# The low halves of eight split weight matrices: subtraction on the engines, or an accumulating DMA

## The chip, the cores and the metric

The kernel runs on one core of a Trainium2 chip. The metric is the time of one execution on the device in microseconds, as the median of several runs. A core has five instruction queues that run side by side and meet only through semaphores: PE (TensorE, matmuls), DVE (VectorE), ACT (ScalarE), POOL (GpSimd) and SP (SyncE, which here only issues DMAs). Each queue is worked off in order, so an instruction that waits holds up everything behind it on its engine. POOL and ACT can issue DMAs too. Sixteen DMA engines carry all transfers.

## The reference

One transformer block on 256 tokens of width 1024, all in float32:

```
h    = rms_norm(x, ln1_g)
proj = h @ w_in                          # 1024 x 4096: u, q, k, v (512 each) and two gates (1024 each)
gate_ssm, gate_attn = split(proj[..., 2048:] + b_gate)
y_ssm  = s5_mixer(u, ...);  g = gelu(y_ssm);  y_ssm = g * sigmoid(g @ w_glu + b_glu)
y_attn = moba_attention(q, k, v, rel_bias)
merged = sigmoid(gate_ssm) * (y_ssm @ w_up_ssm) + sigmoid(gate_attn) * (y_attn @ w_up_attn)
x = x + merged @ w_out
x = x + hier_moe(rms_norm(x, ln2_g), ...)   # 32 experts of 1024 x 512 x 1024, top 2
out = rms_norm(x, ln_f_g)
```

The change touches the product that makes the two gates: the last 2048 columns of `w_in`.

## The kernel before

The 4096 columns of `w_in` are cut into 16 units of 256 columns. A unit's raw weights lie in memory as 128 partitions x 8 x 256 (partition, k, column), 1 MB, and come by one DMA on SP's queue into one of two buffers (`raw`). Units 0 to 7 (u, q, k, v) are multiplied as plain float32 (`nat`). Units 8 to 15, the gates, are split: `wh` is the weights rounded to the short float32r format, `wl` is the rest, raw minus `wh`. The activations are split in the same way (`hH`, `hL`). PE then adds three products for each of the 8 k, `wh*hH`, `wh*hL` and `wl*hH`, which together are nearly as exact as float32. For a half unit (128 columns, part b) that is 24 matmuls: first 16 with `wh`, alternating, then 8 with `wl`. So `wl` is wanted last in every half.

`wh` and `wl` have two buffers each (`wtiles`), so unit u+1 is split while unit u is multiplied. In `half_split`, called for part 0 and part 1 of the unit before, one part is one cast and one subtraction of [128, 8, 128], 1024 elements in each partition. A table (`KN["e"]`) says which engine does which: the casts (`w8.0h` and so on) lie on ACT and DVE, the subtractions (`w8.0l`) on POOL nine times and on DVE seven times. Another table (`KN["sp"]`) says before which quarter of the unit's matmuls the split is written down. The program writes every instruction by hand in one order; an engine's queue is that order with the other engines' instructions left out.

Between the quarters three background threads are advanced (`bg()`): the state-space layer (S5, names `scan`, `W1e`, `M1s`, `Thp`, `yp`, `stp`), its preparation on POOL (`E`, `pprep`, `Pe`) and attention (`attA`, `attB`, `sc`, `ptp`, `pv`), and behind these the gelu. All are finished before the GLU product, which stands between unit 14 and unit 15. After unit 15 come the up projections, the output projection, the routing, and then the experts: 192 pieces of 1 MB of expert weights (`wslot`) run through 21 buffers, and 32 tokens' places of four experts are multiplied at a time. SP issues the pieces in order, each as soon as its buffer is free; the first ones already while the gate units run (`pump`).

Line 691 is the cast in the helper `copy`, line 694 the subtraction in the helper `tt`, line 1269 the matmuls of the gate units, 1108 and 1110 the state-space output, 1070 the state matmuls, 1361 the attention transposes, 1425 the GLU, 1395 to 1405 the gelu.

Of the kernel before, what the change touches and what calls it, by code (L numbers as in the profile page):

```python
# [11 lines left out]
F32R = mybir.dt.float32r  # L12
# [3 lines left out]
AF = mybir.ActivationFunctionType  # L16
OP = mybir.AluOpType
# [5 lines left out]
KD = 8  # L23
# [622 lines left out]
def hybrid_block(ctx, tc, x_ch, x_tok, small, consts, bc, w_in, w_glu, w_up, w_out, rel, onehot, w_rt, w13, w2,  # L646
                 ln_f, out, dbg=None):
    nc = tc.nc
    V, A, G, T, DS = nc.vector, nc.scalar, nc.gpsimd, nc.tensor, nc.sync
# [9 lines left out]
    def blk(i, name, dt=F32):  # L659
        return blocks.tile([128, 2048], dt, tag=f"r{i}", name=name)  # L660

    def carve(t, *shapes):
        res, o = [], 0
        for sh in shapes:
            n = int(np.prod(sh))
            v = t[:, o:o + n]
            names = "abcdef"[:len(sh)]
            if len(sh) > 1:
                v = v.rearrange("p (%s) -> p %s" % (" ".join(names), " ".join(names)), **dict(zip(names, sh)))
            res.append(v)  # L670
            o += n
        assert o <= t.shape[1]
        return res
# [11 lines left out]
    def pick_engine(name, default, opts):  # L685
        OPTS[name] = (default, opts)
        return engines[KN["e"].get(name, default)]

    def copy(name, out_, in_, default="A", opts="AV"):
        e = pick_engine(name, default, opts)  # L690
        (A.copy if e is A else e.tensor_copy)(out_, in_)  # L691

    def tt(name, out, in0, in1, op, default="V", opts="VG"):
        pick_engine(name, default, opts).tensor_tensor(out=out, in0=in0, in1=in1, op=op)  # L694
# [13 lines left out]
    def split(name, raw, wh, wl, scale=None, psum=False):  # L708
        if scale is None:
            copy(name + "h", wh, raw, opts="AV" if psum else "AVG")  # L710
            tt(name + "l", wl, raw, wh.bitcast(F32), OP.subtract, opts="V" if psum else "VG")
        else:
            A.activation(out=wh, in_=raw, func=AF.Copy, scale=scale)
            V.scalar_tensor_tensor(out=wl, in0=raw, scalar=scale, in1=wh.bitcast(F32), op0=OP.mult, op1=OP.subtract)
# [25 lines left out]
    def wtiles(*shape):  # L740
        i = n_w[0] % 2
        n_w[0] += 1
        return carve(blk(4 + i, "wh", F32R), shape)[0], carve(blk(6 + i, "wl", F32R), shape)[0]
# [40 lines left out]
    native = set(("in", u) for u in KN["nat"])  # L784
# [463 lines left out]
    whl = {}  # L1248
    thg = []

    def in_split(u, part):
        if ("in", u) in native:
            return
        if part == 0:
            whl[u] = wtiles(KD, 256)
        wh, wl = whl[u]
        raw = raws["in", u]
        c = slice(part * 128, part * 128 + 128)
        split("w%d.%d" % (u, part), raw[:, :, c], wh[:, :, c], wl[:, :, c])

    def in_mm(ps, u, b, part):
        c = slice(b * 128, b * 128 + 128)
# [199 lines left out]
    def half_split(unit, b):  # L1462
        kind, u = unit
        if kind == "in":
            in_split(u, b)
        elif kind == "glu":
            if b == 0:
                whl["glu"] = wtiles(4, 512)
            wh, wl = whl["glu"]
            c = slice(b * 256, b * 256 + 256)  # L1470
            split("glu.%d" % b, raws["glu"][:, :, c], wh[:, :, c], wl[:, :, c])
        else:
            if b == 0:
                whl[unit] = wtiles(2, 4, 256) if kind == "up" else wtiles(2, DM)
            wh, wl = whl[unit]
            t = (1 - b) if kind == "up" else b
            raw = raws[unit]
            for i in range(2):
                if kind == "up":
                    c = slice(2 * i, 2 * i + 2)  # L1480
                else:
                    c = slice(512 * i, 512 * i + 512)
                split("%s%d.%d.%d" % (kind, u, b, i), raw[:, t, c], wh[:, t, c], wl[:, t, c])
# [19 lines left out]

    s5_angles()
    in_split(1, 0)
    in_split(1, 1)
    vexp(mag, lr, V)
    next_raw()
# [38 lines left out]
    for i, (kind, u) in enumerate(units):  # L1547
# [25 lines left out]
        for b in range(2):  # L1573
# [29 lines left out]
            else:  # L1603
                cb = 2 * u + b
                c = slice(b * 128, b * 128 + 128)
                wh, wl = whl["up", u]
# [103 lines left out]
    for b in range(2):  # L1710
        V.scalar_tensor_tensor(out=em[:, b].rearrange("p (g e) -> p g e", g=4),
                               in0=gsel[:, b].unsqueeze(2).to_broadcast([128, 4, 8]), scalar=NEG,
# [284 lines left out]
```

## Time and profile before

| | |
|---|---|
| median of 3 runs | 683.86 us (681.91 to 684.39) |
| the profiled execution | 681.85 us, its span 680.0 us |
| mean granted clock of TensorE | 0.86 |
| busy: PE, DVE, POOL, ACT | 527.6, 221.7, 159.0, 123.9 us |
| moved by DMA | 235.02 MB, 346 GB/s over the span |

The span begins with the first and ends with the last instruction. Busy times are of the whole span, and most of DVE's, POOL's and ACT's lies in its first 230 us. "Idle before" in a timeline is the time that the engine stood still ahead of the row, with what ended it. A row with x8 merges eight instructions; its duration runs from the start of the first to the end of the last.

### The profile page before, as it was taken

Reading aid. Unit: us, or ns where it says so; the run is one execution under the profiler, and the core shown is the slowest. Engines: PE = TensorE matmul, PEld = TensorE weight load, DVE = VectorE, ACT = ScalarE, POOL = GpSimd, SP = SyncE. Lnnn points to the kernel's source line nnn. Section 1 sums busy time; section 2 is a strip of 40 time slices with the busy share of each in tenths; the row PEclk is TensorE's granted clock in tenths of the full one; section 3 lists DMA queues with packets and bytes.
Section 4 is the critical chain, followed back from the end, with each engine's and each line's share of the span. In section 5 each row is a group of like instructions: output and inputs, shape, how many; then the busy total and the mean of one; then the engine's idle time right before and its main releaser. Section 6 shows DMA issues by size and latency. Waiting matters only on the chain. (4 is left out here: it accounts for less than half of the span.)

```text
span 680.0 us, 9687 instructions
## 1 busy us (share of the span) xinstructions
PE 527.6 (78%) x3947; PEld 294.6 (43%) x3947; DVE 221.7 (33%) x436; ACT 123.9 (18%) x274; POOL 159.0 (23%) x278
## 2 busy tenths in 40 slices
PE   9999879989999789785677757777766776776670
PEld 8787779788988434250032015103301410330030
DVE  4766898868785322110011011101201110120012
ACT  3262554563314110000010000001000000100021
POOL 6898774695772000000000000000000000000020
PEclk9999988997999799988698587866977976697686
DMA  7536444763889999999999999999999999999981
GB/s 270 211 116 193 133 151 147 286 240 142 309 317 420 384 425 419 422 420 423 421 419 422 421 423 421 420 423 422 419 421 422 420 419 424 420 421 421 421 333 67
DMA packets 35155, 235.02 MB, mean 346 GB/s; under 512 B 4052, under 2 KB 5245, under 8 KB 7453
## 3 DMA queue, kind: packets, MB, share of 16 engines
q1 hardware_dynamic: 34700, 232.51, 84.2%
q0 software_dynamic: 256, 1.74, 0.9%
q8 instruction: 33, 0.54, 0.3%
q10 hardware_dynamic: 144, 0.06, 0.1%
q14 instruction: 22, 0.17, 0.1%
HBM read 233.23 MB, written 2.63 MB: 347 GB/s over the span
## 5 line engine op out<-in xcount | busy, mean ns | idle before, releaser
L1807 PE MATMUL pb<-wslot,xg 128*32 128x512 f32 x512 | 92.4, 804 | 44.2 <-DMA wslot<-in_w 44.2
L1807 PE MATMUL pa<-wslot,xg 128*32 128x512 f32 x512 | 87.2, 761 | 34.2 <-DMA wslot<-in_w 34.1
L1887 POOL TENSOR_TENSOR ob<-x,xg 128x256 f32<-128x256 f32 (+1 forms) x6 | 5.3, 910 | 438.6 <-DMA wslot<-in_w 434.3
L1854 PE MATMUL py<-wslot,mt 128*32 128x256 f32 x1024 | 71.0, 420 | 24.9 <-DMA wslot<-in_w 19.4
L1840 DVE SCALAR_TENSOR_TENSOR mt<-mt,pa 128x512 f32<-128x512 f32 x8 | 5.5, 688 | 227.7 <-ACT mt L1839 227.7
L1807 PEld LDWEIGHTS pb<-wslot,xg 128*32 128x32 f32 x512 | 13.0, 122 | 115.3 <-DMA wslot<-in_w 105.2
L1854 PEld LDWEIGHTS py<-wslot,mt 128*32 128x32 f32 x1024 | 31.5, 118 | 64.4 <-DMA wslot<-in_w 31.0
L1807 PEld LDWEIGHTS pa<-wslot,xg 128*32 128x32 f32 x512 | 12.0, 119 | 99.4 <-DMA wslot<-in_w 88.3
L694 POOL TENSOR_TENSOR wl<-raw,wh 128x512 fp32r<-128x512 f32 (+1 forms) x25 | 46.4, 1863 | 29.5 <-ACT wh L691 14.5
L1790 DVE TENSOR_TENSOR xg<-xgp,sm 128x512 f32<-128x512 f32 (+1 forms) x18 | 11.4, 632 | 92.4 <-PE xgp L1788 92.4
L1870 DVE TENSOR_TENSOR x<-x,scp 128x512 f32<-128x512 f32 (+1 forms) x34 | 22.3, 656 | 55.8 <-PE scp L1869 55.8
L1265 PE MATMUL inp<-h,raw 128*128 128x256 f32 x160 | 36.1, 380 | 1.3 <-DVE vu L1284 1.1
L1869 PE MATMUL scp<-mt 128*128 128x512 f32 (+1 forms) x68 | 31.3, 583 | 7.3 <-ACT mt L1866 7.3
L1839 ACT ACTIVATE mt<-pa 128x512 f32<-128x512 f32 x8 | 4.8, 597 | 174.9 <-PE pa L1807 174.9
L1788 PEld LDWEIGHTS xgp<-mt,h 128*128 128x128 f32 x256 | 33.5, 214 | 6.3 <-issue 5.5
L1788 PE MATMUL xgp<-mt,h 128*128 128x128 f32 x256 | 35.5, 302 | 0.9 <-DVE mt L1780 0.9
L1269 PE MATMUL inp<-hH,wh 128*128 128x256 f32 x128 | 34.0, 299 | 1.4 <-DVE wh L691 1.4
L1269 PE MATMUL inp<-hL,wh 128*128 128x256 f32 x128 | 32.7, 289 | 0.0
L1265 PEld LDWEIGHTS inp<-h,raw 128*128 128x128 f32 x160 | 29.8, 190 | 6.2 <-DVE vu L1284 1.8
L1866 ACT COPY mt<-py 128x512 f32<-128x512 f32 (+1 forms) x17 | 9.5, 560 | 125.7 <-PE py L1854 125.7
L694 DVE TENSOR_TENSOR wl<-raw,wh 128x512 fp32r<-128x512 f32 (+1 forms) x25 | 27.6, 1112 | 6.5 <-ACT wh L691 5.6
L1269 PEld LDWEIGHTS inp<-hH,wh 128*128 128x128 f32 x128 | 25.4, 199 | 2.2 <-DVE wh L691 1.6
(324 smaller groups left out, 755.5 us busy)
## 6 DMA issues: line engine op xcount, KB each, us to landing
wslot<-in_w SPq DMA_DIRECT2D x191, 1024.0 KB, 19.8
raw<-in_w_in SPq DMA_DIRECT2D x14, 1024.0 KB, 4.9
raw<-in_w_up SPq DMA_DIRECT2D x4, 1024.0 KB, 5.5
raw<-in_w_out SPq DMA_DIRECT2D x4, 1024.0 KB, 5.4
rbz<-rbd POOLq DMA_DIRECT2D x1, 1536.0 KB, 8.4
xc<-in_x_ch SPq DMA_DIRECT2D x4, 256.0 KB, 5.0
raw<-in_w_in SPq DMA_DIRECT2D x4, 256.0 KB, 5.4
raw<-in_w_in SPq DMA_DIRECT2D x2, 512.0 KB, 7.4
```

What stands on the lines that cost most here:

```text
L694: pick_engine(name, default, opts).tensor_tensor(out=out, in0=in0, in1=in1, op=op)
L1265: T.matmul(ps[:, 0:S], raws["in", u][:, k, c], h32[:, k], start=(k == 0), stop=(k == KD - 1))
L1269: T.matmul(ps[:, 0:S], (wh if x else wl)[:, k, c], (hH if y else hL)[:, k], start=first, stop=last)
L1788: T.matmul(ps[:, i * 128:i * 128 + 128], h2[:, b, k * 128:k * 128 + 128], Dt[:, b].rearrange("p e s -> p (e s)"), start=(b == 0), stop=(b ...
L1790: V.tensor_tensor(out=xg[:, ks[0]:ks[0] + n], in0=ps[:, 0:n * 128].rearrange("p (k n) -> p k n", k=n), in1=smc("g2", ks[0], ks[0] + n).uns ...
L1807: T.matmul(pab[t][32 * e:32 * e + 32], xg[:, k, 32 * e:32 * e + 32], w[:, e], start=(k == 0), stop=(k == KD - 1))
L1840: V.scalar_tensor_tensor(out=hid, in0=hid, scalar=1.0, in1=pab[0], op0=OP.add, op1=OP.mult)
L1854: T.matmul(py[32 * e:32 * e + 32, n % 2 * 256:n % 2 * 256 + 256], hidT[:, f, 32 * e:32 * e + 32], w[:, i, e], start=(f == 0), stop=(f == 3))
L1866: A.copy(ye[:, o % 512:o % 512 + m], py[:, o % 512:o % 512 + m])
L1869: T.matmul(ps[:, 0:m], DwT[:, b], ye[:, o % 512:o % 512 + m], start=True, stop=True)
L1870: V.tensor_tensor(out=x2[:, b, o:o + m], in0=x2[:, b, o:o + m], in1=ps[:, 0:m], op=OP.add)
L1887: G.tensor_tensor(out=ob[:, b, o:o + m], in0=x2[:, b, o:o + m], in1=lnf[:, o:o + m], op=OP.mult)
```

## The change

Only `in_split` is changed, the split of the gate units 8 to 15. Everything is now made in part 0, and part 1 does nothing. The two pieces are no longer halves of the columns but halves of k (four k, all 256 columns, again 1024 elements in each partition). For each piece `wh` is cast as before, on the engine that the table names. `wl` is first filled with the raw weights times -1, rounded to float32r (which is the negated `wh`), on ACT, since the table has no entry for the new names and their default is ACT. Then a DMA on POOL's queue reads the raw weights from memory once more and adds them onto `wl`. The subtraction is gone.

```
-        if ("in", u) in native:
+        if ("in", u) in native or part == 1:
             return
-        if part == 0:
-            whl[u] = wtiles(KD, 256)
-        wh, wl = whl[u]
+        whl[u] = wh, wl = wtiles(KD, 256)
         raw = raws["in", u]
-        c = slice(part * 128, part * 128 + 128)
-        split("w%d.%d" % (u, part), raw[:, :, c], wh[:, :, c], wl[:, :, c])
+        for i in range(2):
+            c = slice(i * 4, i * 4 + 4)
+            copy("w%d.%dh" % (u, i), wh[:, c], raw[:, c], opts="AV")
+            if pick_engine("w%d.%dn" % (u, i), "A", "AV") is A:
+                A.activation(out=wl[:, c], in_=raw[:, c], func=AF.Copy, scale=-1.0)
+            else:
+                V.tensor_scalar(out=wl[:, c], in0=raw[:, c], scalar1=-1.0, scalar2=None, op0=OP.mult)
+            G.dma_start(wl[:, c], w_in[u][:, c].bitcast(F32R), accum_op=OP.add)
```

In the queues the change looks as follows. The numbers behind the names are the program's buffer numbers.

On POOL, where units 10 and 11 are split (`wl_1020` before is unit 11's low half, `wl_786` unit 9's; `pprep`, `Pe` are the preparation for the second half of the state-space layer, `scan` its scan), the queue before was:

```order
L694 TENSOR_TENSOR wl_786<-raw_649,wh_785 128x8x128
L1002 TENSOR_TENSOR pprep_135<-s5a_75,fs_98 128x256
L1003 TENSOR_TENSOR pprep_135<-s5a_75,fs_98 128x256
L983 TENSOR_TENSOR Pe_136<-pprep_135 64x4x4x16 x2
L1002 TENSOR_TENSOR pprep_135<-s5a_75,fs_98 128x256
L1003 TENSOR_TENSOR pprep_135<-s5a_75,fs_98 128x256
L985 TENSOR_TENSOR pprep_135<-pprep_135 128x256
L694 TENSOR_TENSOR wl_1020<-raw_889,wh_1019 128x8x128
L694 TENSOR_TENSOR scan_134<-scan_134 128x256 x2
```

And the same place now (`wl_788` is unit 9, `wl_922` unit 10, `wl_1026` unit 11; line 1263 is the accumulating DMA):

```order
L1263 DMA wl_788<-in_w_in 128x1024 x2
L1263 DMA wl_922<-in_w_in 128x1024 x2
L1002 TENSOR_TENSOR pprep_135<-s5a_75,fs_98 128x256
L1003 TENSOR_TENSOR pprep_135<-s5a_75,fs_98 128x256
L983 TENSOR_TENSOR Pe_136<-pprep_135 64x4x4x16 x2
L1002 TENSOR_TENSOR pprep_135<-s5a_75,fs_98 128x256
L1003 TENSOR_TENSOR pprep_135<-s5a_75,fs_98 128x256
L985 TENSOR_TENSOR pprep_135<-pprep_135 128x256
L1263 DMA wl_1026<-in_w_in 128x1024 x2
L694 TENSOR_TENSOR scan_134<-scan_134 128x256 x2
```

Two DMAs of unit 10 now stand ahead of the preparation, which had no counterpart on POOL before (unit 10's subtractions were DVE's), and both DMAs of unit 11 ahead of the scan.

On ACT, where unit 14 is split (`wh_1353` before, `wh_1365` and `wl_1366` now; `attB` is the last softmax, line 1346 before and 1350 now, and its scaling, line 1352 and 1356), the queue before was:

```order
L1298 ACTIVATE thg_1298<-thg_1298,fs_98 128x256
L691 CAST wh_1353<-raw_1173 128x8x128
L1346 ACTIVATE attB_563,fs_98<-attB_563,fs_98 128x128 x4
L1352 ACTIVATE attB_563<-attB_563,fs_98 128x128 x4
L1298 ACTIVATE thg_1298<-thg_1298,fs_98 128x256
L691 CAST wh_1353<-raw_1173 128x8x128
```

And now:

```order
L1302 ACTIVATE thg_1312<-thg_1312,fs_98 128x256
L691 CAST wh_1365<-raw_1183 128x1024
L1260 ACTIVATE wl_1366<-raw_1183 128x1024
L691 CAST wh_1365<-raw_1183 128x1024
L1260 ACTIVATE wl_1366<-raw_1183 128x1024
L1350 ACTIVATE attB_563,fs_98<-attB_563,fs_98 128x128 x4
L1356 ACTIVATE attB_563<-attB_563,fs_98 128x128 x4
L1302 ACTIVATE thg_1312<-thg_1312,fs_98 128x256
```

The second cast has moved ahead of the softmax, and two negating copies (line 1260) with it.

## Rows read from the trace of the kernel before

**Rows 1.** Windows: busy us of PE, PEld, DVE, ACT, POOL, then PEclk, DMA share, GB/s.

```profile
230.00:232.00 2.00, 2.00 (x17) 0.51 (x10) 0.00 (x0) 0.00 (x0) 0.00 (x0) 0.83 0.64 266
...
231.00:655.00 424.00, 307.96 (x2330) 100.55 (x2318) 48.60 (x91) 22.78 (x43) 0.00 (x0) 0.82 1.01 420
```

**Rows 2.** PE's timeline, its gaps: start, duration, instruction, [idle before <- what ended it].

```profile
86.45 0.55 PE L1108 MATMUL yp<-Thp,Uy 128*32 128x128 f32 x5 [3.27 <-DVE Thp L691]
...
121.86 0.39 PE L1269 MATMUL inp<-hH,wh 128*128 128x256 f32 x1 [1.36 <-DVE wh L691]
...
152.92 0.38 PE L1425 MATMUL glp<-gHL,wh 128*128 128x256 f32 x1 [1.24 <-DVE gHL L691]
```

**Rows 3.** Groups of DVE, ACT, POOL at 68 to 171: busy, mean ns, idle before.

```profile
L694 DVE TENSOR_TENSOR wl<-raw,wh 128x1024 fp32r<-128x1024 f32 x9 | 12.2, 1369 | 0.5 <-ACT wh L691 0.4
...
L691 ACT CAST wh<-raw 128x1024 fp32r<-128x1024 f32 x11 | 11.4, 1038 | 0.0
...
L694 POOL TENSOR_TENSOR wl<-raw,wh 128x1024 fp32r<-128x1024 f32 x9 | 23.3, 2598 | 16.0 <-PE inp L1269 6.2 <-ACT wh L691 4.3 <-DVE wh L691 2.2
```

**Rows 4.** DMA issues: queue, count, size of one, median us to landing.

```profile
raw<-in_w_in SPq DMA_DIRECT2D x14, 1024.0 KB, 4.9
...
rbz<-rbd POOLq DMA_DIRECT2D x1, 1536.0 KB, 8.4
...
mt<-in_w_rt POOLq DMA_DIRECT2D x1, 144.0 KB, 2.5
```

**Rows 5.** POOL's timeline: preparation, first gelu operation, a DMA issue.

```profile
93.70 0.81 POOL L1002 TENSOR_TENSOR pprep<-s5a,fs 128x256 f32<-128x256 f32 x1
...
98.26 0.73 POOL L985 TENSOR_TENSOR pprep<-pprep 128x256 f32<-128x256 f32 x1
...
140.35 0.62 POOL L1395 TENSOR_TENSOR gel<-Uy 128x256 f32<-128x256 f32 x1
...
156.35 0.62 POOL L1561 DMA_DIRECT2D mt<-in_w_rt  x1
```

**Rows 6.** Timelines of DVE and POOL: one DVE operation alone, and beside POOL's.

```profile
79.16 0.42 DVE L694 TENSOR_TENSOR Thp<-scan 128x252 f32<-128x252 f32 x1
...
113.68 2.71 POOL L694 TENSOR_TENSOR wl<-raw,wh 128x1024 fp32r<-128x1024 f32 x1 [4.33 <-ACT wh L691]
...
114.18 2.48 DVE L694 TENSOR_TENSOR Thp<-scan 128x252 f32<-128x252 f32 x1
```

**Rows 7.** Timelines of DVE, PE and ACT around unit 8.

```profile
73.81 0.69 DVE L691 CAST wh<-raw 128x1024 fp32r<-128x1024 f32 x1 [1.56 <-DMA raw<-in_w_in]
...
79.45 1.12 PE L1269 MATMUL inp<-hH,wl 128*128 128x256 f32 x8
...
85.99 0.71 ACT L691 COPY W1e<-pprep 64x192 f32<-64x192 f32 x2 [5.17 <-POOL pprep L985]
```

**Rows 8.** Timelines of ACT and PE around unit 9.

```profile
86.73 1.04 ACT L691 CAST wh<-raw 128x1024 fp32r<-128x1024 f32 x1
...
91.23 0.66 PE L1361 MATMUL ptp<-co,attB 128*128 128x128 f32 x4
```

**Rows 9.** Timelines of ACT and PE around units 10 and 11.

```profile
103.05 0.80 ACT L691 COPY Pe<-pprep 64x256 f32<-64x256 f32 x2
...
112.80 1.90 PE L1070 MATMUL stp<-Uy,M1s 128*128 128x64 f32 x16
```

**Rows 10.** Timelines of PE and ACT around units 13 and 14.

```profile
134.23 1.12 PE L1269 MATMUL inp<-hH,wl 128*128 128x256 f32 x8
...
136.63 1.03 ACT L691 CAST wh<-raw 128x1024 fp32r<-128x1024 f32 x1
...
141.34 0.60 PE L1361 MATMUL ptp<-co,attB 128*128 128x128 f32 x4
```

**Rows 11.** Timelines of ACT and PE around unit 15.

```profile
155.18 0.40 ACT L691 CAST gHL<-gel 128x256 fp32r<-128x256 f32 x1 [3.56 <-DVE gel L1405]
...
166.32 1.12 PE L1269 MATMUL inp<-hH,wl 128*128 128x256 f32 x8
```

## The prediction

> **What bounds the kernel now.** I read first the table of windows, then PE's timeline for its gaps, then the timelines of the engines named as releasers. From 231 to 655 us the DMA engines are busy throughout at 420 GB/s [rows 1]: the expert stage is a stream of weights, and it keeps its length whatever happens before it. Its slots are filled ahead, and just before PE frees the first of them the stream runs dry for a moment: 0.64 busy at 230 to 232 us [rows 1]. So what the stage before takes longer or shorter, the end takes longer or shorter, one to one. The change lies in that earlier stage, in the eight gate units (8 to 14 at 77 to 152 us, 15 behind the GLU at 164 us). There PE is nearly always busy; its gaps are 3.27 us before the state-space output, 1.36 us for a high half in unit 12 and 1.24 us before the GLU [rows 2]. A cost that fits in front of such a gap is free, and a saving is worth no more than the gaps.
>
> **What goes.** Sixteen subtractions of 128x1024: nine on POOL, seven on DVE. In the groups they are 2598 ns each on POOL (23.3 us in all) and 1369 ns on DVE, where nine are counted because two belong to the GLU weights, which stay [rows 3]: 7 x 1.37 = 9.6 us. There is a hidden part: a DVE operation of 0.42 us took 2.48 us where it ran beside such a POOL subtraction [rows 6].
>
> **What comes.** Sixteen negating copies of 128x1024, all on ACT, and sixteen DMAs of 512 KB on POOL's queue. The trace has no negating copy; ACT's plain cast of the same shape takes 1.04 us [rows 3]. I take 1.0, so 16 us more on ACT. Issuing a DMA occupies POOL 0.62 us [rows 5]. No accumulating DMA is in the trace. Its landing is bounded by POOL's own transfers, 2.5 us for 144 KB and 8.4 us for 1536 KB; I take 4.9 us, the landing of a 1024 KB load [rows 4], since 512 KB of source and 512 KB of old contents have to be read. The Trainium skill, page "DMA: Bandwidth & Descriptors", section "Anatomy of one DMA — SWDGE (gpsimd) path", gives about 2.0 us + bytes/436e3 for POOL's DMAs, which would be an estimate of 3.2 us here if the accumulation were free; no run here shows it yet. By it the sum below would stay the same, and only the slower case would lose weight.
>
> **What moves.** Both halves of a split are now cut by k and made during the first half of the unit before. ACT therefore gets three or four operations in one place where one or two stood, and everything behind them in ACT's queue waits. POOL's DMAs wait for ACT, and everything behind them in POOL's queue waits too. I follow this through the four places where it can reach PE.
>
> *Unit 8.* ACT stands at the raw weights, which land at 73.81 us [rows 7]. Negate, cast, negate end at 76.8; the DMAs issue at 74.9 and 76.9 and land at 79.8 and 81.8. PE wants the first at 79.45 [rows 7] and the second four matmuls later, so PE stops about 2 us, but then it had to stop 3.27 us for the state-space output anyway until 86.45 [rows 2]. Free, with about 1.4 us to spare. ACT's own lateness, its stop for the raw weights and the three operations less what it idled there before, goes largely into the 5.17 us that it idled before 85.99 [rows 7], and POOL, which it waited for there, is earlier without its subtractions.
>
> *Unit 9.* At 86.73 ACT had one cast before the second softmax [rows 8]; now it has four operations, 3.0 us more. The softmax gates the transposes on PE at 91.23 [rows 8]: up to 3.0 us late there.
>
> *Units 10 and 11.* The two DMAs of unit 10 stand in POOL's queue ahead of the preparation that ran from 93.70 to 98.99 [rows 5], 5.3 us of work. ACT's negations for unit 10 follow PE's late transposes and end at about 100.6; POOL is free at 101.2 and done at 106.5. ACT copies what POOL prepared, at 103.05 before [rows 9], now at 106.5: 3.4 us late. Behind that copy stand the three operations of unit 11 and the copies that PE's state matmuls at 112.80 need [rows 9]; these had 1 to 2 us of slack, and I put PE 1.9 us late. DVE, which no longer runs into POOL's subtractions, gives back part: the gap of 1.36 us at 121.86 [rows 2] closes, and PE starts unit 12 about 1.0 us late.
>
> *Units 13 and 14.* Unit 13's second DMA issues at 130.6 and lands at 135.5; PE wants it at 134.23 [rows 10] + 0.5 + 1.0 = 135.7. Just hidden. At 136.63 ACT had one cast before the last softmax [rows 10]; now four operations, +3.0 us, less what DVE's earlier scores give back: the transposes at 141.34 [rows 10] start at 143.8, +2.4 us. From there PE took 152.92 - 141.34 = 11.6 us to the GLU, of which 1.24 were a wait [rows 2]; without it PE arrives at 154.1, +1.2 us. POOL issues unit 14's second DMA at 140.8, so the gelu chain starts at 141.4 instead of 140.35 [rows 5]: +1.1 us if it keeps its length, less if POOL gains from a calmer DVE. Either way the GLU is 0 to 1.2 us late.
>
> *Unit 15.* Behind the last gelu cast at 155.18 [rows 11] ACT now does 4.0 us of work: with the chain at +1.1 the second negation ends at 160.7, its DMA lands at 165.6, and PE wants it at 166.32 [rows 11] + 0.5 + 1.1 = 167.9. Hidden, with 2.3 us to spare.
>
> **Sum.** The four places overlap rather than add: what is left at the end is the GLU's 0 to +1.2 us. I take the middle, +0.6. The profiled execution took 681.85 us (span 680.0 and 1.85 around it), so 682.4 in its own terms. The median of the runs is 683.86, 2.0 above that execution; the forecast for the median is 683.86 + 0.6 = 684.5. With landing at 2.5 us the sum is the same. With 8.4 us unit 15's last DMA comes 3.5 us later, 1.2 us beyond what is spare, and unit 13's 3.3 us: up to +3. If all gel work on POOL gains and nothing else is late, -2. That is the range of this case alone: 682 to 687.
>
> **Rivals.**
> *Slower: the landing of the accumulating DMA sets the pace.* PE takes the low half in the last third of each half unit and its queue is in order, so a landing that is later than the slack stops everything. The slack is 1.4 us at unit 8, 0.2 at unit 13, 2.3 at unit 15; it decides from a landing of about 7 us. For it: the read, the addition and the write are all new, and plain transfers on POOL's queue have taken 8.4 us [rows 4]. Against it: a load of 1024 KB in the same stage lands in 4.9 us [rows 4]. At 12 us, about 7 more than I take, unit 15 costs 4.8 us, units 8 and 13 5 to 7 each, of which the later one swallows part: +5 to +12, so 689 to 696.
> *Faster: POOL and DVE were the limit.* POOL loses 23.3 us less 16 x 0.62, and DVE 9.6 us and the stretched operations. The three gaps in rows 2 all end with DVE. If they close and ACT's additions fall into its idle time, 3.3 + 1.4 + 1.2 = 5.9 us go: 678. Against it: at units 9 and 14 ACT is directly on the way to PE. The Trainium skill, page "SBUF — State Buffer", section "Who interferes with whom", says that a DVE operation with two SBUF inputs contends with a POOL operation that reads SBUF, which is what the pair 2.48 against 0.42 us shows; by it the saving on DVE is real, and by the same section a DMA issue on POOL can be held up by DVE's copies, which would take part of it back. No row here shows the second.
> *The change does little because ACT had room.* That is my forecast with the lower end, and is counted there.
>
> **How the numbers follow.** A kernel like this can't be told from no change within about 0.5%, 3.4 us. The forecast's own case has 0.47, nearly all of it within that bound. The landing rival, with the same queueing worked out too small on ACT and POOL, has 0.32, mostly above 687.3. The faster rival has 0.21, mostly below 680.4. Shared out: faster 0.21, same 0.46, slower 0.33. The range runs from the faster rival's 678 to the upper part of the slower one, 695.
>
> **What would show it.** The negating copies at 1.0 us on ACT; the landing of the 512 KB DMAs near 5 us; no wait of PE on low halves above 2 us except in unit 8; the transposes of units 9 and 14 about 2 to 3 us late on PE; the GLU's first matmul at 152.5 to 154.5 us; the stretched DVE operations gone; the expert stage unchanged at 420 GB/s. Landings above 8 us, or a GLU start after 157 us or before 149 us, would prove the forecast wrong.

## The result, and the profile after

The changed kernel takes 709.85 us (median of 4 runs, 707.29 to 711.17) against 683.33 us before, measured beside it (4 runs): ratio 1.0385, 95% interval 1.0349 to 1.0421. It is slower by 26.5 us. The forecast was 684.5 us with a range up to 695; the measurement lies outside it, further out than the slower rival went.

The profiled execution took 707.29 us with a span of 705.5. The windows of the kernel after, with the columns of [rows 1]: the expert stream, and the front from 70 us to the first matmul of the up projection.

```profile
70.00:197.30 127.30, 95.16 (x848) 87.62 (x847) 63.69 (x122) 67.86 (x147) 54.00 (x84) 0.83 0.80 229
...
258.00:682.00 424.00, 310.48 (x2324) 101.42 (x2321) 48.63 (x91) 22.80 (x43) 0.00 (x0) 0.81 1.01 420
```

The expert stream runs at 420 GB/s as before, 424 us of it. All of the loss lies in the front. In the kernel before, the same stretch is this window:

```profile
70.00:170.16 100.16, 88.69 (x844) 82.54 (x843) 84.88 (x128) 50.57 (x127) 67.13 (x76) 0.93 0.50 186
```

The stretch grew by 27.1 us. In it ACT's busy time rose from 50.57 to 67.86 us and DVE's fell from 84.88 to 63.69, POOL's from 67.13 to 54.00: the load has moved to ACT, as the change says. PE's matmuls are the same, 844 and 848 records. PE's busy time grew by 95.16 - 88.69 = 6.5 us, with the granted clock down from 0.93 to 0.83; the rest, 20.7 us, is time in which PE stands. The DMA engines' share went from 0.50 to 0.80.

PE's timeline after shows where it stands; the column in brackets is the idle time and what ended it. These answer to [rows 2]:

```profile
81.55 0.74 PE L1273 MATMUL inp<-hH,wl 128*128 128x256 f32 x4 [1.03 <-DMA wl<-in_w_in]
87.42 1.22 PE L1273 MATMUL inp<-hH,wl 128*128 128x256 f32 x4 [5.12 <-DMA wl<-in_w_in]
102.24 0.74 PE L1273 MATMUL inp<-hH,wl 128*128 128x256 f32 x4 [0.98 <-DMA wl<-in_w_in]
...
123.62 0.74 PE L1273 MATMUL inp<-hH,wl 128*128 128x256 f32 x4 [2.27 <-DMA wl<-in_w_in]
127.41 1.22 PE L1273 MATMUL inp<-hH,wl 128*128 128x256 f32 x4 [3.06 <-DMA wl<-in_w_in]
150.93 1.22 PE L1273 MATMUL inp<-hH,wl 128*128 128x256 f32 x4 [6.04 <-DMA wl<-in_w_in]
155.93 1.23 PE L1273 MATMUL inp<-hH,wl 128*128 128x256 f32 x4 [3.77 <-DMA wl<-in_w_in]
...
173.79 1.06 PE L1429 MATMUL glp<-gHL,wh 128*128 128x256 f32 x5
...
189.72 1.22 PE L1273 MATMUL inp<-hH,wl 128*128 128x256 f32 x4 [6.73 <-DMA wl<-in_w_in]
192.24 1.22 PE L1273 MATMUL inp<-hH,wl 128*128 128x256 f32 x4 [1.31 <-DMA wl<-in_w_in]
```

Nine waits for a low half end with the accumulating DMA, a pair each in units 8, 11, 13 and 15 and one in unit 9; together they are 30.3 us. They swallowed gaps of before, which is part of why 30.3 us of waits make only 20.7 us more of standing: the 3.27, the 1.36 and the 1.24 us of [rows 2] are gone, and so is most of a fourth gap, which the prediction's list leaves out. It stood in front of the state matmuls, was ended by ACT's copies for them (`M1s`), and is 1.06 us after:

```profile
102.53 1.55 PE L1070 MATMUL stp<-Uy,M1s 128*128 128x64 f32 x12 [2.92 <-ACT M1s L691]
```

The pairs are the two transfers of a unit, wanted four matmuls apart.

The transfers themselves, by queue and by issue (queue: packets, MB, share of 16 engines; issue: count, KB each, median us to landing), answer to [rows 4]; then the new operations on ACT and POOL, which answer to [rows 3]:

```profile
q0 software_dynamic: 2560, 10.13, 7.4%
...
raw<-in_w_in SPq DMA_DIRECT2D x14, 1024.0 KB, 8.9
wl<-in_w_in POOLq DMA_DIRECT2D x16, 512.0 KB, 10.6
...
raw<-in_w_glu SPq DMA_DIRECT2D x1, 1024.0 KB, 14.8
```

```profile
L1260 ACT ACTIVATE wl<-raw 128x1024 fp32r<-128x1024 f32 x16 | 16.5, 1051 | 7.7 <-DMA raw<-in_w_in 7.7
L1263 POOL DMA_DIRECT2D wl<-in_w_in x16 | 14.4, 932 | 28.6 <-ACT wl L1260 19.9 <-PE m1p L1044 8.6
```

The low halves land after 10.6 us, not 4.9, and they slow their neighbours: a raw load takes 8.9 us where it took 4.9 [rows 4]. POOL's queue held 0.9% of the 16 engines' span before (256 packets) and holds 7.4% now; 0.074 x 705.5 - 0.009 x 680 = 46 us, so by an estimate from these shares each of the 16 transfers keeps all 16 engines about 2.9 us busy. At the stream's 420 GB/s, 512 KB would be 1.25 us.

How a landing becomes 10 to 15 us can be read in one place, unit 13. First SP's issues, then POOL's, from the timelines after:

```profile
134.41 0.81 SPq L766 DMA_DIRECT2D wslot<-in_w  x2
135.32 0.36 SPq L731 DMA_DIRECT2D raw<-in_w_in  x1
135.73 0.70 SPq L766 DMA_DIRECT2D wslot<-in_w  x1
140.86 0.33 SPq L731 DMA_DIRECT2D raw<-in_w_glu  x1
```

```profile
140.19 1.81 POOL L1263 DMA_DIRECT2D wl<-in_w_in  x2 [4.01 <-ACT wl L1260]
...
149.17 0.86 POOL L1263 DMA_DIRECT2D wl<-in_w_in  x1 [5.24 <-ACT wl L1260]
...
151.98 0.61 POOL L1399 TENSOR_TENSOR gel<-Uy 128x256 f32<-128x256 f32 x1
```

From 134.41 us on SP issues five loads of 1 MB (2.5 us each at 420 GB/s, 12.5 us) and POOL two low halves (2.7 us each, below, 5.4 us): 17.9 us of work for the 16 engines, and the second low half lets PE go at 155.93, 21.5 us after the first of these issues; unit 14's first transfer came in between. The engines are full all that time (a DMA share of 0.98 from 134.41 to 155.93), at fewer bytes. Two windows of this time after, and the same two before:

```profile
140.00:150.00 10.00, 4.89 (x42) 4.43 (x41) 2.82 (x8) 9.89 (x23) 4.28 (x8) 0.91 1.02 342
150.00:160.00 10.00, 5.30 (x64) 4.57 (x68) 0.67 (x3) 4.08 (x14) 4.32 (x8) 0.50 1.04 293
```

```profile
140.00:150.00 10.00, 9.17 (x81) 8.71 (x81) 9.58 (x13) 5.93 (x14) 9.39 (x12) 1.00 0.69 265
150.00:160.00 10.00, 7.21 (x35) 5.95 (x34) 6.47 (x12) 3.78 (x8) 6.86 (x13) 0.78 0.39 153
```

At 140 to 150 us ACT is at 9.89 of 10 us and DVE at 2.82. At 150 to 160 the granted clock is 0.50 on average, the lower level of 1.2 GHz, right behind the wait of 6.04 us; four matmuls take 1.22 us there, where eight took 1.12 before [rows 10], so a wait costs a second time in the matmuls that follow. The gelu chain that began at 140.35 [rows 5] begins at 151.98.

### The profile page after: what moved, and what is told of

It reads as the page before. It is cut to its first block, busy times and chain, and to the rows that moved or that the text cites. A ratio compares the mean times of both kernels' runs of the same rounds, so it can differ in the third digit from the quotient of the medians.

```text
span 705.5 us, 9729 instructions
## 1 busy us (share of the span) xinstructions
PE 535.7 (76%) x3947; PEld 300.1 (43%) x3947; DVE 200.0 (28%) x429; ACT 139.0 (20%) x290; POOL 145.7 (21%) x285
## 2 busy tenths in 40 slices
DMA packets 37459, 243.42 MB, mean 345 GB/s; under 512 B 4307, under 2 KB 5500, under 8 KB 9756
## 5 line engine op out<-in xcount | busy, mean ns | idle before, releaser
L1811 PE MATMUL pb<-wslot,xg 128*32 128x512 f32 x512 | 94.6, 822 | 45.0 <-DMA wslot<-in_w 44.8
L1811 PE MATMUL pa<-wslot,xg 128*32 128x512 f32 x512 | 85.4, 746 | 34.6 <-DMA wslot<-in_w 34.6
L1858 PE MATMUL py<-wslot,mt 128*32 128x256 f32 x1024 | 73.9, 435 | 21.2 <-DMA wslot<-in_w 15.7
L1811 PEld LDWEIGHTS pa<-wslot,xg 128*32 128x32 f32 x512 | 12.1, 120 | 99.4 <-DMA wslot<-in_w 87.8
L1273 PE MATMUL inp<-hH,wl 128*128 128x256 f32 x128 | 23.2, 319 | 30.3 <-DMA wl<-in_w_in 30.3
L1273 PE MATMUL inp<-hH,wh 128*128 128x256 f32 x128 | 37.1, 318 | 0.0
L1273 PE MATMUL inp<-hL,wh 128*128 128x256 f32 x128 | 35.7, 307 | 0.0
L1792 PE MATMUL xgp<-mt,h 128*128 128x128 f32 x256 | 33.9, 293 | 0.9 <-DVE mt L1784 0.9
L1792 PEld LDWEIGHTS xgp<-mt,h 128*128 128x128 f32 x256 | 31.9, 205 | 5.9 <-issue 5.1
L1273 PEld LDWEIGHTS inp<-hH,wl 128*128 128x128 f32 x128 | 19.2, 215 | 32.4 <-DMA wl<-in_w_in 32.4
L1273 PEld LDWEIGHTS inp<-hH,wh 128*128 128x128 f32 x128 | 28.2, 220 | 0.7 <-issue 0.5
## 6 DMA issues: line engine op xcount, KB each, us to landing
wl<-in_w_in POOLq DMA_DIRECT2D x16, 512.0 KB, 10.6
```

Source lines behind the costliest of these rows:

```text
L1273: T.matmul(ps[:, 0:S], (wh if x else wl)[:, k, c], (hH if y else hL)[:, k], start=first, stop=last)
L1792: T.matmul(ps[:, i * 128:i * 128 + 128], h2[:, b, k * 128:k * 128 + 128], Dt[:, b].rearrange("p e s -> p (e s)"), start=(b == 0), stop=(b ...
L1811: T.matmul(pab[t][32 * e:32 * e + 32], xg[:, k, 32 * e:32 * e + 32], w[:, e], start=(k == 0), stop=(k == KD - 1))
L1858: T.matmul(py[32 * e:32 * e + 32, n % 2 * 256:n % 2 * 256 + 256], hidT[:, f, 32 * e:32 * e + 32], w[:, i, e], start=(f == 0), stop=(f == 3))
```

## The experiments

Theory 1: the accumulating transfer is dear in itself. Theory 2: it stands in line with SP's loads for the same 16 engines, and a cheap transfer would come late too. Theory 3 (the rival that leaves the transfer out): the copies that ACT took over and the in-order queues of ACT and POOL make the loss. All times below are medians; the kernel before, measured beside them, had medians of 682.3 to 683.2 us. "Up" is the first matmul of the up projection on PE (170.2 us before, 197.3 after); from it to the end of the span it is 508 to 511 us in every run below that makes the whole block on the same weights, except in the two with the stream held back.

**The transfers alone.** A kernel that only moves gate weights, one kind at a time, each kind after the one before has landed, the whole series twice. Some of its cases in outline:

```
fence(); accum(half)                 fence(); loads(); accum(half); accum(half)
fence(); plain(half)                 fence(); loads(); plain(half); plain(half)
# loads(): two 1 MB loads on SP; fence(): POOL reads one element of every tile
```

> No part of the reference: the transfers alone, one kind at a time on an idle chip, each twice (the output is zeros). Theory 1: an accumulating 512 KB transfer lands 7 us or more after its issue with nothing beside it, a plain one from the same queue in 3 to 5 us, one from SP in about 3 us; two at once land later by their own time of 2.5 us or more each. Theory 2: alone the accumulating one lands in under 5 us, as the plain one does; behind two 1 MB loads of SP both kinds land after about 8 to 10 us.

POOL's timeline; a copy of g from acc (or pln) starts when the transfer has landed. Accumulating alone, plain alone, two accumulating, two plain, then both kinds behind SP's loads:

```profile
17.76 1.00 POOL L683 DMA_DIRECT2D acc<-in_w_in  x1
23.45 0.43 POOL L673 COPY g<-acc 128x1 f32<-128x1 f32 x2 [4.69 <-DMA acc<-in_w_in]
...
26.28 0.55 POOL L686 DMA_DIRECT2D pln<-in_w_in  x1
...
30.23 0.43 POOL L673 COPY g<-pln 128x1 f32<-128x1 f32 x2 [2.97 <-DMA pln<-in_w_in]
...
52.55 0.18 POOL L673 COPY g<-acc 128x1 f32<-128x1 f32 x1 [3.71 <-DMA acc<-in_w_in]
55.30 0.18 POOL L673 COPY g<-acc 128x1 f32<-128x1 f32 x1 [2.56 <-DMA acc<-in_w_in]
...
62.08 0.18 POOL L673 COPY g<-pln 128x1 f32<-128x1 f32 x1 [2.66 <-DMA pln<-in_w_in]
63.32 0.18 POOL L673 COPY g<-pln 128x1 f32<-128x1 f32 x1 [1.05 <-DMA pln<-in_w_in]
...
78.25 1.77 POOL L683 DMA_DIRECT2D acc<-in_w_in  x2
86.96 0.18 POOL L673 COPY g<-acc 128x1 f32<-128x1 f32 x1 [6.93 <-DMA acc<-in_w_in]
89.42 0.18 POOL L673 COPY g<-acc 128x1 f32<-128x1 f32 x1 [2.27 <-DMA acc<-in_w_in]
...
92.25 1.09 POOL L686 DMA_DIRECT2D pln<-in_w_in  x2
...
100.38 0.18 POOL L673 COPY g<-pln 128x1 f32<-128x1 f32 x1 [6.60 <-DMA pln<-in_w_in]
```

Alone the accumulating 512 KB lands after 23.45 - 17.76 = 5.7 us, the plain one after 4.0. The second of a pair comes 55.30 - 52.55 = 2.75 us after the first, a plain one 63.32 - 62.08 = 1.24. I read this as the engines' own time, 191 against 423 GB/s. It is one reading of several: in the second series the accumulating pair was 3.56 us apart, and behind SP's loads 2.46 (89.42 - 86.96) and 2.44, so 2.4 to 3.6 us; the plain pair was 1.23 apart again. The float32r format of the target is not what makes it dear: into a plain float32 tile the transfer lands after 5.5 us, the plain one after 4.1. Behind SP's loads the first lands after 8.7 us accumulating and 8.1 plain. These two can't be set against each other: SP issued its loads 3.2 and 0.7 us ahead of the accumulating transfer, and 1.1 and 0.7 us ahead of the plain one, which so had more in front of it. Neither theory has it whole. The landing alone is no 7 us (against theory 1), but the engines' time is about double (against theory 2), and the line adds to both.

**The changed kernel without its transfers**, in two forms. With the copies left at -1:

```diff
-            G.dma_start(wl[:, c], w_in[u][:, c].bitcast(F32R), accum_op=OP.add)
```

> The changed kernel without its 16 accumulating transfers: the negating copies, the cut by k and both halves in part 0 stay; the low parts are then only the negated weights (the addition is left out). Theory 1 (the transfer is dear in itself) and theory 2 (it is as cheap as a plain one but stands in line with SP's loads) both take the whole loss to hang on the landing: 678 to 690 us, and no wait of TensorE for a low half over 2 us. Theory 3 (ACT's extra copies and the in-order queues of ACT and POOL make the loss, the transfer is a bystander): most of the 26 us stays, 700 us or more.

781.95 us (ratio 1.1451, 1.1426 to 1.1477), but this is no price of the transfers: with such low parts other tokens meet at the experts and the weights of one more pass are loaded (261.5 MB moved, 243.4 in the changed kernel). Its front can be read: up at 165.5 us. So the copies were scaled by 0 as well, which leaves the routing alone:

```diff
-                A.activation(out=wl[:, c], in_=raw[:, c], func=AF.Copy, scale=-1.0)
+                A.activation(out=wl[:, c], in_=raw[:, c], func=AF.Copy, scale=0.0)
```

> The changed kernel without its 16 accumulating transfers, and with the copies scaled by 0 instead of -1, so that the low parts are zero and the routing of the tokens stays as it is (the low parts are left out). All that the change does on ACT, DVE and POOL is there, only the transfers and the wait for them are gone. Transfers make the whole loss (theories 1 and 2): the up projection starts near 166.5 us, as in the run with the negated copies alone, and the time is 677 to 681 us, some 4 us under the kernel before. If part of the loss sits on the engines (theory 3): 690 us or more.

677.80 us, ratio 0.9920 (0.9888 to 0.9951), up at 166.6. PE's two longest gaps between 70 us and the up projection, from its timeline (two more are 0.82 and 0.86 us):

```profile
93.81 1.09 PE L1364 MATMUL ptp<-co,attB 128*128 128x128 f32 x4 [5.34 <-DVE attB L694]
...
141.98 0.69 PE L1364 MATMUL ptp<-co,attB 128*128 128x128 f32 x4 [1.76 <-DVE Uy L1116]
```

The engines' part of the change is a gain of 4.5 us, ACT's 16 copies included. So ACT's copies do not make the loss, and theory 3 falls for them; the transfers and all that waits for them cost 709.85 - 677.80 = 32 us. With the transfers go their issues on POOL (14.4 us) and POOL's waits ahead of them (28.6 us idle, 19.9 of it for ACT), so this run does not part POOL's queue from the transfers. What speaks for the transfers is PE's timeline, where all 30.3 us of waits end with a landing; how much of a late landing is a late issue on POOL, no run shows. The attention transposes of units 9 and 14, where I expected ACT to be late, are the gaps that are left (5.34 and 1.76 us, ended by DVE). They start 2.6 and 0.6 us later than before; 3.0 and 2.4 were forecast.

**The same transfers without the addition** (the low parts are then the raw weights).

```diff
-            G.dma_start(wl[:, c], w_in[u][:, c].bitcast(F32R), accum_op=OP.add)
+            G.dma_start(wl[:, c], w_in[u][:, c].bitcast(F32R))
```

> The changed kernel with the 16 transfers made plain: same bytes, same queue, same places, no addition (the low parts are then the raw weights). Theory 1: a plain transfer lands in about 5 us, the waits for the low halves shrink to a few us in all, 684 to 695 us; the 16 DMA engines' share of GpSimd's queue falls from 7.4% to about 4%. Theory 2: the same bytes wait in the same line, so the landing stays near 10 us and the time at 703 to 712 us. Theory 3: 703 to 712 us too.

695.87 us (ratio 1.0177, 1.0155 to 1.0198), up at 185.9. POOL's queue and the landing:

```profile
q0 software_dynamic: 2560, 10.13, 4.6%
...
wl<-in_w_in POOLq DMA_DIRECT2D x16, 512.0 KB, 7.7
```

This run moves the same 243.42 MB as the changed kernel and takes as long from up to the end (508 us), so its wrong low parts don't disturb the comparison. In the middle between the theories: of the 32 us, the bytes on the line cost 18 (695.87 - 677.80) and the addition, which keeps the engines longer for the same bytes (2.9 us against 1.6 by the queue's shares) and POOL longer for an issue, 14.

**The cut and the earlier place alone**, with the subtractions on engines that had them.

```diff
...
+        for i in range(2):
+            c = slice(i * 4, i * 4 + 4)
+            split("w%d.%d" % (u, i), raw[:, c], wh[:, c], wl[:, c])
```

> The kernel before with the two halves of a unit cut by k and both made in part 0, as the changed kernel has them, but with the subtractions kept on the engines that had them (no negating copy, no transfer). If the earlier place and the cut cost nothing, as theories 1 and 2 have it: 678 to 690 us. If making both halves in one go holds up ACT, DVE and POOL (theory 3): 690 us or more, with longer waits for stp, yp and ptp.

685.61 us, ratio 1.0036 (1.0023 to 1.0049): 2.4 us slower. Against the run with zero low parts, which differs from it by the subtractions and has the copies more, the subtractions are worth 685.61 - 677.80 = 7.8 us, the copies already paid. The faster rival's relief is real: its 5.9 us were for the whole change on the engines, and of that 4.5 us came, as the cut and the earlier place take 2.4 back.

**The stream held back.** The six pieces of 1 MB that go out inside the gate units are issued in the first up unit; once in the changed kernel and once in the kernel before, as the price of holding. The entries of the table, put in one line:

```diff
-       'in9.0': 1, 'in11.1': 2, 'in12.1': 1, 'in14.0': 1, 'in15.1': 1, 'up0.0': 0,
+       'in9.0': 0, 'in11.1': 0, 'in12.1': 0, 'in14.0': 0, 'in15.1': 0, 'up0.0': 6,
```

> The changed kernel with the six 1 MB pieces of the expert stream that are issued inside the gate units held back to the first up unit. Theory 2 (the landing is late because SP's megabytes stand in the same line): the landing falls from 10.6 to about 8 us, the waits for low halves in units 12, 13 and 15 shrink from 22 us to under 10, and the up projection starts before 190 us instead of at 198. Theory 1 (the transfers' own 2.7 us each set the pace, with or without the stream): landing within 1 us of 10.6, up projection at 195 to 199 us. The end by theory 2: about 700 us, as six pieces come later but the front is earlier; by theory 1: 708 us or more.

> The kernel before with the same six pieces held back to the first up unit: the price of holding them. The stream is the bound and each piece is 2.5 us, so if all six are loaded 15 us later into time that was full: up to 698 us; where the DMA engines still had free time from the up units on: 683 to 690 us. The start of the up projection stays at 171 us either way.

The changed kernel: 701.21 us (ratio 1.0268, 1.0219 to 1.0317), up at 183.8, landing 9.6 us. The kernel before: 696.28 us (1.0185, 1.0146 to 1.0223). Half of the 27 us in the front (13.5) goes away when SP has six megabytes less to load beside the transfers, which theory 1 alone can't give. The waits for low halves fall from 30.3 to 22.2 us, in units 11, 13 and 15 from 23.2 to 10.9 (the expectation's unit 12 should read 11), and PE's busy time in the front by 4. Of the 13.5 us only 8.6 are left at the end, because the held pieces are late there: in the kernel before, whose up stays at 170.2, PE waits 9.99 us inside the up projection for weights behind them. But the landing fell by 1 us only, less than expected; the raw weights, 1 MB per unit, stay in the line, with the other half of the pair.

**Three units only.** The kernel before with both transfers of units 9, 11 and 14. The expectation calls them units without a wait; that was misread, as the rows above show: of the three it holds for 14 alone. The casts of these units stand on ACT here; one of the six was DVE's.

```diff
+        if u in (9, 11, 14):
+            if part == 0:
+                for i in range(2):
...
+                    A.activation(out=wl[:, c], in_=raw[:, c], func=AF.Copy, scale=-1.0)
+                    G.dma_start(wl[:, c], w_in[u][:, c].bitcast(F32R), accum_op=OP.add)
+            return
```

> The kernel before with accumulating transfers in units 9, 11 and 14 alone, the three in which TensorE never waited for a low half in the changed kernel; the other units subtract as before. If a unit's transfer costs only where its landing is late, and these three are hidden: 680 to 685 us, no wait for a low half over 1 us. If every transfer slows SP's loads beside it (theory 1 and 2 both allow it) and the chain feels it: 686 to 695 us.

686.89 us, ratio 1.0050 (1.0030 to 1.0070). The median landing is 9.3 us with six transfers, hardly less than with sixteen. PE waits 0.51, 3.53 and 3.52 us, the last at 157.55 in unit 14, where it had not waited in the changed kernel: there the 9.8 us lost in unit 13 had covered it. The median hides two kinds: the first transfers of units 9 and 11 land after 5.7 us, as alone, and the other four after 9.0 to 12.1. What these four have beside them are SP's loads, ahead of them or just behind, and three of them also the first of their pair. One of the two that take 12.1 us is the second transfer of unit 11. POOL's timeline, then SP's:

```profile
111.14 0.87 POOL L1264 DMA_DIRECT2D wl<-in_w_in  x1 [1.03 <-ACT wl L1263]
```

```profile
111.39 0.33 SPq L766 DMA_DIRECT2D wslot<-in_w  x1
111.77 0.98 SPq L731 DMA_DIRECT2D raw<-in_w_in  x2
```

PE's wait for it ends at 123.24, 12.1 us after the issue. That is 6.4 us more than alone; the first of the pair, 1.9 us ahead, can take about its own 2.75 of them, and the rest is left to SP's 3 MB, which were issued 0.3 to 1.2 us behind it. So a load needn't be ahead of a transfer to delay it.

**Half the bytes, and an earlier start.** The second half of k by transfer, made first, the first half by a subtraction on DVE; then units 8, 9 and 11 to 14 started up to three quarters of a unit earlier; then both.

```diff
-        for i in range(2):
+        for i in (1, 0):
...
+            if i == 0:
+                V.tensor_tensor(out=wl[:, c], in0=raw[:, c], in1=wh[:, c].bitcast(F32), op=OP.subtract)
+                continue
# earlier start:
-       'in7.0': 1, 'in8.0': 3, 'in10.0': 1, 'in11.0': 2, 'in12.0': 2, 'in13.0': 3,
+       'in7.0': 0, 'in8.0': 0, 'in10.0': 0, 'in11.0': 0, 'in12.0': 0, 'in13.0': 0,
```

> Half the bytes: in each unit the second half of k is made first, by a negating copy and the accumulating transfer, and the first half by a subtraction on VectorE (8 transfers, 4.2 MB). If the loss goes with the bytes (theory 1, every transfer costs its own 2.7 us of the engines): about half of it, 692 to 697 us. If it is the line that counts (theory 2: a wait only where the landing passes the slack of 2 to 5 us that a unit has): landing about 7 us, waits for low halves under 8 us in all, 681 to 690 us.

> The changed kernel with the making of units 8, 9, 11, 12, 13 and 14 started one to three quarters of a unit earlier, at the first quarter of the unit before. If only lead is missing (the DMA engines have time to spare over a unit): each of the six gets 1 to 3 us of lead, the waits for low halves fall from 30 us to 15 to 20 us and the time to 695 to 702 us. If the DMA engines are full over a unit (10 us of transfers in 10 us of matmuls) or the raw weights land no earlier: 706 to 712 us, with ACT waiting longer for raw weights.

> Both at once: half the bytes and the earlier start. If lead and bytes each do what the two runs beside it claim, hardly a wait for a low half is left, and with GpSimd and VectorE relieved of half of the subtractions the time is at or a little under the kernel before, 679 to 685 us. If the transfers slow SP's loads whatever their number: 686 to 692 us.

Half: 691.43 us (ratio 1.0138, 1.0083 to 1.0194). Early: 706.66 us (1.0352, 1.0298 to 1.0406). Both: 692.92 us (1.0168, 1.0110 to 1.0226). The earlier start helps hardly at all: ACT then waits longer for the raw weights (20.7 us in all, 7.7 after), and the line is as full. With half the bytes the loss over the zero run is 13.6 of 32 us, the eight subtractions that stay on DVE included. The median landing is the 5.7 us of a transfer alone, yet the waits for low halves are 12.5 us in all, more than the 8 expected. Two short ones are 1.74 and 0.59 us; the two long ones, in PE's timeline of that run:

```profile
142.00 1.22 PE L1276 MATMUL inp<-hH,wl 128*128 128x256 f32 x4 [4.50 <-DMA wl<-in_w_in]
...
174.38 1.22 PE L1276 MATMUL inp<-hH,wl 128*128 128x256 f32 x4 [5.70 <-DMA wl<-in_w_in]
```

The second, in unit 15, shows the line and POOL's queue at once. POOL's timeline, then SP's:

```profile
162.97 1.34 POOL L1569 TENSOR_TENSOR mt<-mt,sm 128x288 f32<-128x288 f32 x1 [1.94 <-DMA mt<-in_w_rt]
...
164.63 0.88 POOL L1266 DMA_DIRECT2D wl<-in_w_in  x1
```

```profile
155.30 8.84 SPq L731 DMA_DIRECT2D raw<-in_w_up  x2
164.19 0.42 SPq L766 DMA_DIRECT2D wslot<-in_w  x1
```

The negated half was there at 161.6 us, but POOL first waited for the router weights; and half a microsecond before the transfer SP had issued 2 MB (the issue of the second of the two at 155.30 ends at 164.14, with that row, and the stream's piece follows at 164.19). Alone it would land after 5.7 us, with 2 x 2.5 us ahead after 10.7; it took 174.38 - 164.63 = 9.8.

**Only where it is hidden.** The kernel before with the second half of k by transfer in units 9, 10, 11, 12 and 14, units 8, 13 and 15 untouched. In the five units all casts stand on ACT; four of them were DVE's.

```diff
+        if u in (9, 10, 11, 12, 14):
+            if part == 0:
...
+                G.dma_start(wl[:, c], w_in[u][:, c].bitcast(F32R), accum_op=OP.add)
+                c = slice(0, 4)
...
+                V.tensor_tensor(out=wl[:, c], in0=raw[:, c], in1=wh[:, c].bitcast(F32), op=OP.subtract)
+            return
```

> The kernel before with the transfer for the second half of k alone, in units 9, 10, 11, 12 and 14 (5 transfers, 2.6 MB); units 8, 13 and 15, whose halves came late in the run with half the bytes, subtract as before. If a transfer costs only where its landing comes after the slack of its unit: no wait for a low half over 1 us, and a little relief of GpSimd: 678 to 683 us. If each transfer costs by its bytes on the DMA engines (some 27 us for 8.4 MB): about 8 us more than before, 688 to 692 us. The run with units 9, 11 and 14 whole (6 transfers, +4.6 us) stands between the two.

685.17 us, ratio 1.0057 (1.0033 to 1.0081). Landing 5.8 us, and no wait for a low half is left. So the price by bytes alone (+8) falls, but there is no gain: PE waits elsewhere, the longest 4.54 us for ACT's copies before the state matmuls (`M1s`). PE's timeline, then DVE's:

```profile
118.34 2.82 PE L1070 MATMUL stp<-Uy,M1s 128*128 128x64 f32 x12 [4.54 <-ACT M1s L691]
```

```profile
110.45 1.23 DVE L1266 TENSOR_TENSOR wl<-raw,wh 128x1024 fp32r<-128x1024 f32 x1 [7.06 <-ACT wh L1265]
```

The trace leads from one to the other: DVE stood 7.06 us until ACT had made the second cast of unit 11, the state scan and the preparation behind this subtraction in DVE's queue came late, ACT stood 2.27 and 1.20 us for them, and its copy for the state matmuls, which is behind, ran at 117.72. The run with the cut alone has a wait at the same place, 2.80 us at 117.22, there too behind ACT's waits for DVE (3.01 and 1.74 us). No version that makes the full low parts beat the kernel before.

## Why the prediction was wrong

- *The term that failed* is the landing: "I take 4.9 us, the landing of a 1024 KB load". As the time of one transfer on an idle chip it was nearly right, 5.7 us. The error was to use it as a constant. The sum counted no DMA engine time for the 16 transfers (an estimate: 16 x 2.75 = 44 us of all 16 engines, in a stretch of 100 us in which they were 0.50 busy: 94 of 100, with loads that come in bursts; with plain transfers the same sum is 70 of 100, and they still cost 18 us). The runs showed in its place a landing that hangs on what SP loads beside it: 5.5 to 14.8 us in the changed kernel, 10.6 in the median, and nine waits of PE, 30.3 us in all, where the sum had about 2, and these inside a gap.
- *Why 512 KB is 2.75 us.* I set it equal to a 1 MB load because of what has to be read; a 1 MB load keeps the engines for 2.5 us, so the guess was fair, but I let it bear on the landing only.
- *The fit of the Trainium skill*, page "DMA: Bandwidth & Descriptors", section "Anatomy of one DMA — SWDGE (gpsimd) path", gave an estimate of 3.2 us. Alone, the plain transfer took 4.0 and the accumulating one 5.7: the slope for plain bytes agrees (1.24 us per 512 KB against 1.20), the fixed part of 2.0 us is 0.8 short here, and the addition is outside it. The prediction's sentence that by this fit the slower case would lose weight pointed the wrong way.
- *Unit 8*: "Free, with about 1.4 us to spare". PE waited 1.03 and 5.12 us, not 2.
- *Unit 13*: "just hidden", slack 0.2 us. It was late by 6.04 and 3.77 us.
- *Unit 15*: "2.3 us to spare". Late by 6.73 and 1.31 us. Here a second step was missing: POOL's queue holds the router weights' load and the operation that waits for it ahead of these transfers; I had the row of that issue [rows 5] and used it for its duration only.
- *ACT's negating copies*: 1.05 us each, taken as 1.0. Right, and they cost nothing. POOL's issue took 0.93 us on average, taken as 0.62 from a DMA of 144 KB.
- *DVE's stretched operations* went, as said: after, the operation of 0.42 us in [rows 6] takes 0.42 us both times. This is a second term that failed: the engines' part is -4.5 us, the forecast had +0.6. Of the 3.6 us by which up comes earlier in the zero run, 2.4 are a shorter busy time of PE (88.69 to 86.24 us at a granted clock of 0.93 and 0.95), which the sum didn't have. The other 1.1 are what the gaps give in all, the 2.92 us that the prediction's list and the faster rival's 5.9 leave out among those that went.
- *The slower rival* had the right mechanism ("a landing that is later than the slack stops everything"). At its landing of 12 us it gave 689 to 696, at 10.6 the chip gave 709.85. It priced three units; in the run there were five, PE was slowed by the lower granted clock behind them (6.5 us), and SP's raw and GLU loads came late too (8.9 and 14.8 us, before 4.9 and 5.3; the GLU load takes 9.4 in the zero run, so not all of it is the transfers).
- *What was right*: the loss or gain of the front goes one to one into the end (+27.1 against +26.5 us), and the expert stream stays at 420 GB/s. The sign that would prove the forecast wrong, landings above 8 us or a GLU start after 157 us, is what came: 10.6 and 173.8.

What stays open: the 18 us of the plain transfers is not split further into landing, slowed raw loads and clock. How much of a late landing is POOL's own lateness is open too, as no run moves the transfers' place in POOL's queue alone. That the run with the transfers hidden loses its 2.3 us by DVE's wait for ACT's cast is read from its trace; no run took that wait away.

## What to carry to other kernels

Before moving work from an engine to a DMA, count it as occupancy of the DMA engines, add every load that is issued in the same few microseconds, and only then compare with the slack; a landing measured alone was about the lower bound here (5.7 us alone, 5.5 to 14.8 in the changed kernel). A DMA share of 0.50 on average doesn't tell whether there is room at the moment that counts: in unit 13 five loads of 1 MB were issued within 6.5 us. Where there was room, in the run with five transfers, no wait for one was left, and still nothing was won. Where two effects of opposite sign are possible, as here a relief of 4.5 us and a price of 32, run the change with the dear part taken out, to see each by itself.

## What the runs showed that I had not expected

- An accumulating DMA of 512 KB keeps the 16 engines 2.75 us (2.4 to 3.6 in four pairs), a plain one on the same queue 1.24 us (191 and 423 GB/s), and its issue holds POOL 0.86 us or more against 0.55.
- Loads on SP and transfers on POOL share the engines so far that a line can be added up to within a microsecond in the one place where I did: 5.7 us alone plus 2.5 us for each megabyte issued just before gives 10.7, measured 9.8. Three loads issued 0.3 to 1.2 us behind another transfer delayed that one as well; it took 12.1 us.
- Unit 14's transfers were hidden in the changed kernel and made PE wait 3.52 us when fewer others came before them: an earlier wait covers a later one, so a place without a wait is no proof of slack.
